# Weight-block sums formed in SBUF at use, instead of once in a DRAM scratch

## The chip, the cores and the metric

The kernel runs on one core of one Trainium2 chip. The metric is the device time of one execution in microseconds (us); lower is better. Three executions of the kernel before gave a median of 2685.73 us (2682.78 to 2697.74 us). A core has a matrix engine (PE, whose weight loads the profile lists apart as PEld), a vector engine (DVE), a scalar engine (ACT), a general engine (POOL), and SP, which here only starts transfers. SP's, ACT's and POOL's transfers run in queues of their own over 16 shared DMA engines.

## The reference

One layer of a decoder, for a prompt of 2048 tokens and 64 sample tokens that share all weights, all in fp32:

```python
x = x + concat([attn_o, pool_o]) @ w_out          # mixer: window attention and pooling heads
h = rmsnorm(x, g_cross); q = (h @ w_cq).reshape(...)
x = x + softmax(q @ mem_k) @ mem_v @ w_co          # cross-attention into 256 memory tokens
h = rmsnorm(x, g_ffn)
x = x + square(relu(h @ w_up)) @ w_down            # feed-forward, width 1024 -> 4096 -> 1024
y = rmsnorm(x, g_final)
```

This case is about the weights `w_up` and `w_down` of the feed-forward.

## The kernel before

**Two halves of the program.** First the mixer and the cross-attention run over the 2112 tokens in three superblocks (`superblock`); their last step, with weights `B`, adds the cross-attention's output. Then the feed-forward (`mlp`) runs over the same tokens in three segments of 704 tokens (`NSEG`, index j). Between the two, x and the normalised h are kept in DRAM (`xq`, `hq`).

**Precision.** A matrix product of fp32 operands is made of three PE products. Each operand is split into a high part, rounded by ACT to the PE's fp32r format, and the rest, which DVE or POOL subtracts; high times high, high times rest and rest times high are summed in PSUM (`mm3`; the three matmuls are lines 148 to 150).

**The feed-forward's products.** A block product of 2 x 2 blocks is done with seven products in place of eight (a Strassen scheme, indices i = 1 to 7). The hidden width is cut into eight groups g. `ups(j, g)` computes the seven up-products of a group, `downs(j, g)` the seven down-products of it; the order is `ups(j, 0)`, then `ups(j, g)`, `downs(j, g-1)` in turn, so a **pair** is seven up- and seven down-products. The eighth group's down-part (`down_last`) uses plain blocks. One product is 24 matmuls. Each of the seven takes a weight tile of 128 x 1024 (512 KB): for i = 3 and 4 a raw block of the weight, for i = 7, 2, 5 and 6 a sum of two blocks, for i = 1 a difference. Activations have such sums too: `hsplit` makes those of the hidden layer, with a POOL addition where one is needed (line 1452), an ACT rounding (line 1455) and a DVE subtraction (line 1456). The two hidden buffers `HC` take turns, so the split for the product after the next waits until PE has finished with its buffer.

**Where the weight tiles come from.** For each of 15 weight groups (8 up, 7 down) the scratch `us_s` or `ds_s` holds all seven tiles. They are made once, by `Work`: six copies DRAM to DRAM on SP's queue (line 1724), four transfers on POOL's queue that add a second block into the copied one (line 1726), and one difference, which is loaded into SBUF, subtracted by DVE (line 1703) and stored. `Work.step` issues the next of these at fixed places of the program: through the second and third superblock, the cross-attention, and on into the first feed-forward segment (after most products with j = 0).

**The stream of weights.** `Stream` hands out weight tiles in the order of use. There are ten SBUF tiles (`WS`), two per item: the raw tile becomes the rest, a second takes the rounded high part. `emit` issues the load (line 174), the ACT rounding (line 175) and the subtraction (line 176, on DVE; on POOL for i = 5 and 1 of the down-products) in one go, up to five items ahead (`pump`), as soon as tiles are given back. Instructions run in order on each engine, so ACT's rounding of a tile stands in ACT's queue from the moment the item is emitted.

**What sets the order.** The program is recorded in Python's order, then a scheduler moves instructions by their dependences; what is wrapped in `keep_in_program_order` keeps its place among its like. The places shown below are read from the built program.

## Time and profile before

| | |
|---|---|
| median of three runs | 2685.73 us (2682.78 to 2697.74) |
| the profiled execution | 2693.55 us, span 2691.8 us |
| PE, DVE, ACT, POOL busy | 92%, 68%, 47%, 29% of the span |
| bytes moved by DMA | 468.26 MB, of them 31.46 MB in POOL's queue |
| transfers POOL issues that add into `us_s`, `ds_s` | 32 and 28 of 512 KB |
| feed-forward segments | three, from about 1256, 1780 and 2236 us; the last runs to the end |

The span is the profiler's, from the first to the last instruction. A row of the stages view gives for a stretch of time the busy time of each engine, in brackets its number of instructions, then the clock that PE was granted as a share of full speed, the share of the 16 DMA engines' time and the rate moved. The timeline gives start, duration, engine, line and, in brackets, how long the engine was idle before and what ended it. In the DMA view a row of issues ends with the median time from issue to landing.

### The profile page before, as it was taken

The page shows a single profiled execution, that of the slowest core. Times are in us where ns is not written, and L with a number is a line of the kernel's source. Part 1 is how long each engine was busy: PE and PEld are TensorE (multiplying, and loading weights), DVE is VectorE, ACT ScalarE, POOL GpSimd, SP SyncE. Part 2 cuts the span into 40 slices and gives each one's busy share as a digit, 9 for nine tenths or more (in the row PEclk, how much of TensorE's full clock was granted, in tenths as well). Part 3 has the DMA queues.
Part 4 walks back from the last instruction along what each step waited for, and adds up shares of the span by engine and source line. Part 5 has one row for each costly group of instructions (what it writes and reads, how often), then busy time and mean ns, then how long its engine had stood idle before and what let it go on. Part 6 is the DMA issues. An engine that isn't in the chain of part 4 may idle for free.

```text
span 2691.8 us, 38281 instructions
## 1 busy us (share of the span) xinstructions
PE 2474.4 (92%) x14655; PEld 2332.1 (87%) x14655; DVE 1840.2 (68%) x2591; ACT 1252.2 (47%) x2055; POOL 788.1 (29%) x713
## 2 busy tenths in 40 slices
PE   7899989679999889997898989899999989999997
PEld 7798868678979779667888979899999989999997
DVE  6568264558455556647667658987787898787787
ACT  5666234337244344434544334545545545544542
POOL 3215224315334224211422312133322214222220
PEclk9999999889999889998999989999999999999998
DMA  7841525763736947476876623463433436433331
GB/s 244 256 143 53 213 102 189 242 192 108 233 123 200 295 135 246 169 276 216 275 225 208 227 94 137 163 206 134 138 137 133 159 125 213 138 135 133 135 140 67
DMA packets 167275, 468.26 MB, mean 174 GB/s; under 512 B 22852, under 2 KB 85252, under 8 KB 161540
## 3 DMA queue, kind: packets, MB, share of 16 engines
q1 hardware_dynamic: 149620, 417.05, 44.2%
q0 software_dynamic: 4800, 31.46, 6.4%
q10 hardware_dynamic: 12672, 17.30, 1.8%
q8 instruction: 115, 1.88, 0.3%
q14 instruction: 68, 0.56, 0.1%
HBM read 417.90 MB, written 135.94 MB: 206 GB/s over the span
## 4 chain that ended last, share of the span: by engine, by line
PE 56%; DVE 20%; DMA 10%; ACT 5%; issue 4%; POOL 3%; SPq 0%; ACTq 0%; DVEq 0%; POOLq 0%
PE d L149 11%; PE d L150 11%; PE d L148 11%; PE mm L337 5%; PE mm L336 5%; PE mm L335 4%; DVE w L176 4%; DVE act L1456 3%; ACT w L175 2%; DMA w<-us_s 2%; DMA w<-ds_s 2%; DVE x L1488 2%; PE mm L150 2%; PE mm L149 2%; PE mm L148 2%
## 5 line engine op out<-in xcount | busy, mean ns | idle before, releaser
L148 PE MATMUL d<-act,w 128*128 128x352 f32 x2552 | 834.4, 328 | 38.1 <-ACT w L175 17.6
L150 PE MATMUL d<-act,w 128*128 128x352 f32 x2552 | 833.4, 327 | 1.9 <-DVE w L176 1.9
L149 PE MATMUL d<-act,w 128*128 128x352 f32 x2488 | 813.0, 327 | 15.1 <-DVE act L1456 14.1
L175 ACT CAST w<-w 128x1024 fp32r<-128x1024 f32 x411 | 430.0, 1049 | 630.5 <-DMA w<-us_s 275.1
L176 DVE TENSOR_TENSOR w<-w,w 128x1024 fp32r<-128x1024 f32 x369 | 497.2, 1350 | 234.7 <-ACT w L175 232.0
L148 PEld LDWEIGHTS d<-act,w 128*128 128x128 f32 x2552 | 485.8, 191 | 45.2 <-ACT w L175 19.5
L149 PEld LDWEIGHTS d<-act,w 128*128 128x128 f32 x2488 | 477.3, 192 | 27.2 <-DVE act L1456 26.0
L150 PEld LDWEIGHTS d<-act,w 128*128 128x128 f32 x2552 | 487.5, 191 | 3.5 <-DVE w L176 3.4
L335 PE MATMUL mm<-act,w 128*128 128x384 f32 (+2 forms) x1248 | 414.9, 333 | 37.5 <-ACT w L175 29.5
L337 PE MATMUL mm<-act,w 128*128 128x384 f32 (+2 forms) x1248 | 410.4, 329 | 3.3 <-DVE w L176 3.1
L336 PE MATMUL mm<-act,w 128*128 128x384 f32 (+2 forms) x1248 | 408.8, 328 | 0.1
L335 PEld LDWEIGHTS mm<-act,w 128*128 128x128 f32 x1248 | 241.7, 194 | 44.5 <-ACT w L175 31.3
L337 PEld LDWEIGHTS mm<-act,w 128*128 128x128 f32 x1248 | 241.8, 194 | 9.8 <-DVE w L176 5.5
L336 PEld LDWEIGHTS mm<-act,w 128*128 128x128 f32 x1248 | 242.0, 194 | 3.1 <-DVE act L701 0.4
L259 POOL TENSOR_TENSOR t<-t,t 128x384 f32<-128x384 f32 (+2 forms) x133 | 149.0, 1122 | 279.2 <-ACT t L258 273.2
L1452 POOL TENSOR_TENSOR fb<-fb 128x704 f32<-128x704 f32 x65 | 131.5, 2029 | 289.1 <-DVE act L1456 269.1
L176 POOL TENSOR_TENSOR w<-w,w 128x1024 fp32r<-128x1024 f32 x42 | 103.1, 2455 | 357.5 <-ACT w L175 357.1
L1488 DVE TENSOR_TENSOR x<-d,x 128x704 f32<-128x704 f32 x210 | 181.6, 883 | 21.4 <-PE d L150 21.3
L1452 POOL TENSOR_TENSOR fr<-fr 128x704 f32<-128x704 f32 x40 | 81.4, 2034 | 148.1 <-DVE act L1456 137.6
L150 PE MATMUL mm<-w,act 128*128 128x512 f32 x288 | 115.8, 402 | 6.7 <-DVE act L290 4.8
L148 PE MATMUL mm<-w,act 128*128 128x512 f32 x288 | 114.9, 403 | 7.4 <-ACT act L288 5.1
L149 PE MATMUL mm<-w,act 128*128 128x512 f32 x288 | 114.8, 399 | 3.5 <-DVE w L176 3.5
(291 smaller groups left out, 3730.9 us busy)
## 6 DMA issues: line engine op xcount, KB each, us to landing
w<-us_s SPq DMA_DIRECT2D x168, 512.0 KB, 3.3
w<-ds_s SPq DMA_DIRECT2D x147, 512.0 KB, 3.2
us_s<-in_wup SPq DMA_DIRECT2D x48, 512.0 KB, 7.2
ds_s<-in_wdn SPq DMA_DIRECT2D x42, 512.0 KB, 7.2
us_s<-in_wup POOLq DMA_DIRECT2D x32, 512.0 KB, 8.2
ds_s<-in_wdn POOLq DMA_DIRECT2D x28, 512.0 KB, 7.1
w<-a_s SPq DMA_DIRECT2D x24, 512.0 KB, 5.1
w<-b_s SPq DMA_DIRECT2D x24, 512.0 KB, 3.6
```

The lines of the kernel that those rows point to most:

```text
L148: nc.tensor.matmul(ps, Wh(k), Hh(k), start=first and i == 0, stop=False)
L149: nc.tensor.matmul(ps, Wh(k), Hl(k), start=False, stop=False)
L150: nc.tensor.matmul(ps, Wl(k), Hh(k), start=False, stop=final and i == last)
L175: i1 = nc.scalar.copy(th[:], r[:, 0:1024])
L176: i2 = eng.tensor_tensor(tl[:], r[:, 0:1024], f32(th[:]), ALU.subtract)
L259: nc.gpsimd.tensor_tensor(self.acc[:, 0:n], self.acc[:, 0:n], t[:, 0:n], ALU.add)
L335: nc.tensor.matmul(ps[:, 0:n], w8(th)[:, k, :], hi(b, k), start=k == 0, stop=False)
L336: nc.tensor.matmul(ps[:, 0:n], w8(th)[:, k, :], lo(b, k), start=False, stop=False)
L337: nc.tensor.matmul(ps[:, 0:n], w8(tl)[:, k, :], hi(b, k), start=False, stop=k == 7)
L1452: nc.gpsimd.tensor_tensor(pre[0], pre[0], pre[1], pre[2])
L1456: nc.vector.tensor_tensor(lo, src, f32(hi), ALU.subtract)
L1488: nc.vector.tensor_tensor(r, v2(d), r, ALU.add)
```

## The change

The scratch now holds four raw blocks per group instead of seven finished tiles. They are copied there once, as are the other scratch weights, by 39 transfers on POOL's queue, two 512 KB blocks at a time, at every other call of `Work.step`; no sum or difference is made ahead, and none of `Work`'s transfers is left in the feed-forward. The feed-forward's items go through a new stage `pipe`: SP loads the first block; at the next `pump` POOL issues a transfer that adds the second block into the SBUF tile (`add_on`); two pumps later the tile is split as before (`split`). For i = 1 both blocks are loaded, into the two tiles of the item, and DVE forms the difference through a scratch of 704 and one of 320 columns (`DT`), ACT rounds it and DVE subtracts. Over the program that is 180 adding transfers into SBUF and 45 second loads. At most two items are held split (`RDY`), six in all (`DEPTH`).

```diff
-WIX = {3: 0, 7: 1, 2: 2, 4: 3, 5: 4, 6: 5, 1: 6}
+WSUM = {3: (0,), 4: (3,), 7: (1, 3), 2: (2, 3), 5: (0, 1), 6: (2, 0), 1: (0, 3)}
+RDY, DEPTH, CAGE = 2, 6, 2
...
-    us_s = drp.tile([8, 7, P, 1024], F32, name="us_s", tag="us_s")
-    ds_s = drp.tile([7, 7, P, 1024], F32, name="ds_s", tag="ds_s")
+    us_s = drp.tile([8, 4, P, 1024], F32, name="us_s", tag="us_s")
+    ds_s = drp.tile([7, 4, P, 1024], F32, name="ds_s", tag="ds_s")
...
             if key[0] in ("us", "ds"):
                 assert work.ready(key[0][0], key[2]), key
+                tl = WS.get()
+                nc.sync.dma_start(f32(tl[:]), raw[0])
+                th = None
+                if key[3] == 1:
+                    th = WS.get()
+                    nc.sync.dma_start(f32(th[:]), raw[1])
+                    raw = raw[:1]
+                self.pipe.append([key, tl, raw[1:], eng, 0, th])
+                return
...
+        def add_on(self, e):
+            for src in e[2]:
+                tc.keep_in_program_order(nc.gpsimd.dma_start(f32(e[1][:]), src, accum_op=ALU.add))
+            e[2] = ()
+
+        def split(self):
+            key, tl, raw, eng, n, th = self.pipe.popleft()
+            if th is not None:
+                for t, c in zip(DT, (slice(0, 704), slice(704, 1024))):
+                    nc.vector.tensor_tensor(t, f32(tl[:, c]), f32(th[:, c]), ALU.subtract)
+                    nc.scalar.copy(th[:, c], t)
+                    nc.vector.tensor_tensor(tl[:, c], t, f32(th[:, c]), ALU.subtract)
+            else:
+                th = WS.get()
+                nc.scalar.copy(th[:], f32(tl[:]))
+                eng.tensor_tensor(tl[:], f32(tl[:]), f32(th[:]), ALU.subtract)
+            self.ready.append((key, th, tl))
+
         def pump(self):
-            while self.items and len(WS.free) - 2 >= self.resW and len(self.ready) < 5:
+            for e in self.pipe:
+                e[4] += 1
+                if e[2]:
+                    self.add_on(e)
+                    e[4] = 1
+            while self.pipe and self.pipe[0][4] > CAGE and len(self.ready) < RDY and WS.free:
+                self.split()
+            while self.items:
+                if self.items[0][0][0] in ("us", "ds"):
+                    if len(WS.free) < 2 + self.resW or len(self.pipe) + len(self.ready) >= DEPTH:
+                        break
...
-                if j == 0 and i not in (3, 6):
-                    work.step()
...
-                cp_ = [("c", o[g, i], w[g, b], None) for i, b in enumerate((0, 1, 2, 3, 0, 2))]
-                ac = [("a", o[g, i], w[g, b], (k, g) if i == 5 else None) for i, b in ((1, 3), (2, 3), (4, 1), (5, 0))]
...
+                self.units += [(o[g, 2 * h:2 * h + 2], w[g, 2 * h:2 * h + 2], (k, g) if h else None) for h in range(2)]
...
         def step(self, go=True):
...
+            if go and self.units:
+                self.odd += 1
+                if self.odd % 2:
+                    self.unit()
```

The built program shows where the new instructions stand. Below, w0 to w9 are the ten weight tiles, act6 and act7 the two hidden buffers, fb and fr the hidden groups, d0 to d3 the PSUM tiles; a wait on DMAHW is one on a transfer that SP issued, on DMASW one that POOL issued. Both places are in the second segment, at `downs` of the fourth group.

ACT, the last five hidden roundings (L1455) of that group and the weight roundings (L175) between them, before:

```order
L1455 CAST act6_66<-fb1_87 128x704 [waits PE_49]
L175 CAST w6_82<-w1_77 128x1024 [waits DMAHW2_49]
L1455 CAST act7_67<-fb1_87 128x704 [waits PE_49]
L175 CAST w4_80<-w8_84 128x1024 [waits DMAHW3_49]
L1455 CAST act6_66<-fb1_87 128x704 [waits DVE_49,PE_49,Pool_49]
L175 CAST w5_81<-w9_85 128x1024 [waits DMAHW4_49,Pool_49]
L1455 CAST act7_67<-fb1_87 128x704 [waits DVE_49,PE_49]
L175 CAST w0_76<-w3_79 128x1024 [waits DMAHW5_49]
L1455 CAST act6_66<-fb1_87 128x704 [waits DVE_49,PE_49,Pool_49]
```

and after the change, the same five (now L1492) with the weight roundings (now L207):

```order
L1492 CAST act6_66<-fb1_87 128x704 [waits PE_49]
L1492 CAST act7_67<-fb1_87 128x704 [waits PE_49]
L1492 CAST act6_66<-fb1_87 128x704 [waits DVE_49,PE_49,Pool_49]
L207 CAST w3_79<-w8_84 128x1024 [waits DMASW5_49,Pool_49]
L1492 CAST act7_67<-fb1_87 128x704 [waits DVE_49,PE_49]
L207 CAST w4_80<-w5_81 128x1024 [waits DMASW6_49,PE_49]
L1492 CAST act6_66<-fb1_87 128x704 [waits DVE_49,PE_49,Pool_49]
L207 CAST w7_83<-w1_77 128x1024 [waits DMAHW6_49,DMASW7_49]
```

Before, a weight rounding that waits for an SP load stands ahead of each hidden rounding. Now two do, and they wait for an adding transfer: those of the down-weights i = 7 (DMASW5) and i = 6 (DMASW6). The third (DMASW7) is the next group's up-weight i = 2.

POOL, from the same group on, before (L1452 hidden additions, L176 weight subtractions):

```order
L1452 TENSOR_TENSOR fb1_87<-fb1_87 128x704 [waits DVE_49,Pool_49] x2
L176 TENSOR_TENSOR w9_85<-w9_85,w5_81 128x1024 [waits DMAHW7_49,PE_49,Activation_49]
L1452 TENSOR_TENSOR fr4_13382<-fr4_13382 128x704 [waits Activation_49] x2
L176 TENSOR_TENSOR w7_83<-w7_83,w2_78 128x1024 [waits DMAHW1_49,PE_49,Activation_49]
L1452 TENSOR_TENSOR fb1_87<-fb1_87 128x704 [waits DVE_49]
```

and after (L195 adding transfers, L1489 hidden additions, L208 a weight subtraction):

```order
L195 DMA w5_81<-ds_s_95 128x1024 [waits DMAHW2_49,DMASW3_49,PE_49]
L195 DMA w3_79<-ds_s_95 128x1024 [waits DMAHW4_49,PE_49]
L1489 TENSOR_TENSOR fr4_13337<-fr4_13337 128x704 [waits Activation_49]
L208 TENSOR_TENSOR w3_79<-w3_79,w9_85 128x1024 [waits DMASW4_49,Activation_49]
L1489 TENSOR_TENSOR fr4_13337<-fr4_13337 128x704 [waits Activation_49]
L195 DMA w8_84<-ds_s_95 128x1024 [waits DMAHW0_49,DMASW5_49,PE_49]
L195 DMA w5_81<-ds_s_95 128x1024 [waits DMAHW1_49,DMASW6_49,PE_49]
L1489 TENSOR_TENSOR fb1_87<-fb1_87 128x704 [waits DVE_49]
L195 DMA w1_77<-us_s_94 128x1024 [waits DMAHW2_49,DMASW7_49,PE_49]
L195 DMA w9_85<-us_s_94 128x1024 [waits DMAHW4_49,DMASW0_49,PE_49]
L195 DMA w5_81<-us_s_94 128x1024 [waits DMAHW0_49,DMASW1_49,PE_49]
```

POOL's queue loses one of its two weight subtractions in a pair and gets eight adding transfers. In the rows shown, ds_s rows are the down-weights i = 2, 5, then 7 and 6; us_s rows the up-weights i = 2, 5 and 7 of the next group. Each waits for its SP load, and the hidden additions stand between them.

More of the change, by code (lines that the diff above doesn't have):

```diff
@@ L1490, in downs @@
                     flush()
-                    if pp == 0 and j == 0 and i != 6:
-                        work.step()
                 WS.put(th, tl)
@@ L1669, in __init__ @@
             grp = [(k, g) for g in range(8) for k in "ud"][:-1]
-            self.units, self.made = [], set()
-            self.diffs = [(us_s if k == "u" else ds_s, io["wup"] if k == "u" else io["wdn"], g) for k, g in grp]
-            one = [("c", win_s[2 * g:2 * g + 2], io["win"][2 * g:2 * g + 2], None) for g in range(5)]
-            one += [("c", wo_s[4 * h:4 * h + 4, :, 0:512], io["woa"][4 * h:4 * h + 4], None) for h in range(2)]
-            prev = []
+            self.made = set()
+            self.units = [(win_s[2 * g:2 * g + 2], io["win"][2 * g:2 * g + 2], None) for g in range(5)]
@@ L1686, in __init__ @@
-                prev = ac
-            self.units += [("c", dn_s[h:h + 1], io["wdl"][h:h + 1], None) for h in range(4)]
-            self.units += prev
-            self.n = 0
-            self.tile = None
-            self.job = None
-            self.more = True
+                self.units += [(o[g, 2 * h:2 * h + 2], w[g, 2 * h:2 * h + 2], (k, g) if h else None) for h in range(2)]
+            self.units += [(dn_s[2 * h:2 * h + 2], io["wdl"][2 * h:2 * h + 2], None) for h in range(2)]
+            self.odd = 0
@@ L1694, in ready @@
         def ready(self, k, g):
-            return (k, g) in self.made and all(not (d[2] == g and d[0] is (us_s if k == "u" else ds_s)) for d in self.diffs)
+            return (k, g) in self.made
         def step(self, go=True):
-            self.n += 1
-            if self.job:
-                (o, w, g), at = self.job
-                t = self.tile
-                if self.n - at == DLAG:
-                    tc.keep_in_program_order(nc.vector.tensor_tensor(t[:, 0:1024], t[:, 0:1024], t[:, 1024:2048], ALU.subtract))
-                elif self.n - at == DLAG + 1:
-                    tc.keep_in_program_order(nc.sync.dma_start(o[g, 6], t[:, 0:1024]))
-                    self.job = None
-                    if not self.more:
-                        self.tile = None
-            elif self.tile is not None and self.diffs and go:
-                x = self.diffs.pop(0)
-                o, w, g = x
-                for i in range(2):
-                    tc.keep_in_program_order(nc.sync.dma_start(self.tile[:, 1024 * i:1024 * i + 1024], w[g, 3 * i]))
-                self.job = (x, self.n)
-                return
```

49 lines of the change are left out of this document (15 added, 34 removed).

## The prediction

> **What bounds the kernel now.** I read the page's busy times and slices first, then the stages view over the feed-forward, then waits and timeline where a stage falls short.
>
> ```profile
> PE 2474.4 (92%) x14655; PEld 2332.1 (87%) x14655; DVE 1840.2 (68%) x2591; ACT 1252.2 (47%) x2055; POOL 788.1 (29%) x713
> PEclk9999999889999889998999989999999999999998
> DMA  7841525763736947476876623463433436433331
> q0 software_dynamic: 4800, 31.46, 6.4%
> ```
>
> PE is busy for 92% of the span, nearly always at its full clock, so time is won only where PE waits. The stages show where (columns: stretch, length, then PE, PEld, DVE, ACT, POOL, then clock, DMA share, GB/s):
>
> ```profile
> 1283.00:1306.00 23.00, 16.04 (x85) 15.29 (x84) 12.75 (x9) 10.10 (x12) 15.08 (x10) 0.85 1.03 341
> 1306.00:1760.30 454.30, 415.80 (x2417) 404.17 (x2416) 334.26 (x338) 204.28 (x240) 117.61 (x69) 0.95 0.55 178
> 1760.30:2214.50 454.20, 444.91 (x2722) 439.06 (x2721) 372.06 (x387) 230.65 (x272) 125.73 (x60) 0.99 0.44 151
> 1400.00:1420.00 20.00, 16.31 (x88) 15.25 (x87) 14.76 (x17) 8.24 (x10) 0.85 (x2) 0.91 0.76 233
> 1540.00:1600.00 60.00, 46.52 (x221) 43.51 (x220) 23.98 (x23) 21.52 (x25) 12.94 (x7) 0.80 0.33 111
> 1555.00:1560.00 5.00, 3.70 (x11) 3.24 (x12) 1.22 (x1) 0.94 (x2) 0.00 (x0) 0.50 0.01 2
> 1720.00:1740.00 20.00, 14.34 (x81) 12.71 (x80) 20.00 (x25) 10.88 (x13) 0.00 (x0) 0.98 0.58 193
> ```
>
> The second and third rows are stretches of equal length in the first and the second segment. The first does 2417 matmuls, the second 2722: 305 x 454.2 / 2722 = 51 us of PE work missing. Ahead of it, 23 us hold 85 matmuls where the second segment's rate gives 138: 9 more. In the second segment, away from the change of segments, nothing is left to win; the sum of fourteen 10-us stages from 1880 to 2020 us reads
>
> ```profile
> sum 140.00, PE 139.72 PEld 138.54 DVE 110.56 ACT 70.30 POOL 39.31; mean PE 9.98 PEld 9.90 DVE 7.90 ACT 5.02 POOL 2.81
> ```
>
> So a pair of 14 products (24 matmuls each, 14 x 24 x 454.2 / 2722 = 56 us with the change of segments in it; 52.5 us at the full rate of 64 in 10 us) is PE's. What the first segment lacks, the timeline shows in one place:
>
> ```profile
> 1398.08 0.32 SPq L174 DMA_DIRECT2D w<-us_s  x1
> 1398.44 0.49 SPq L1724 DMA_DIRECT2D us_s<-in_wup  x1
> 1402.03 1.04 ACT L175 CAST w<-w 128x1024 fp32r<-128x1024 f32 x1 [7.01 <-DMA w<-ds_s]
> 1402.98 0.77 ACT L1455 CAST act<-fb 128x704 fp32r<-128x704 f32 x1
> ```
>
> ACT stood 7.01 us in a weight's rounding, behind it the hidden rounding that PE's next product needed, with a scratch copy between the loads on SP's queue. The waits view says how common that is over the run (time, count, mean), and the DMA view of 1290 to 1560 us, against that from 1780 us on, how much slower a load lands beside the copies:
>
> ```profile
> ACT w L175 <- DMA w<-us_s: 275.1, 131, 6.9
> ```
>
> ```profile
> q1 hardware_dynamic: 9989, 48.57, 48.4%
> q0 software_dynamic: 1680, 11.01, 21.4%
> w<-us_s SPq DMA_DIRECT2D x30, 512.0 KB, 4.6
> us_s<-in_wup POOLq DMA_DIRECT2D x11, 512.0 KB, 8.3
> ds_s<-in_wdn POOLq DMA_DIRECT2D x10, 512.0 KB, 7.9
> ```
>
> ```profile
> q1 hardware_dynamic: 43735, 129.30, 41.2%
> w<-us_s SPq DMA_DIRECT2D x106, 512.0 KB, 3.2
> ```
>
> **A, the first segment.** 25 copies and 25 adding transfers leave it, and its load landings should fall from 4.6 to 3.2 us. At most the whole 60 us come back. At least none, since the row of 1540 to 1600 us loses much with almost nothing of the copies left: 221 matmuls where the second segment's rate gives 360, so 60 x 139 / 360 = 23 us, with the 16 engines a third busy and at 1555 idle (0.01). Whether that slow stretch is an after-effect of the copies the rows don't show. I take the other 60 - 23 = 37 whole and a third of the 23: **-45**.
>
> **B, the mixer.** Its chain of waits has writes and loads that take far longer than their like (start, length):
>
> ```profile
> 521.34 7.55 DMA xq<-x
> 539.04 19.65 DMA xq<-x
> 562.77 15.46 DMA hq<-x
> 867.86 8.24 DMA w<-win_s
> 905.38 10.90 DMA hq<-x
> 944.75 8.32 DMA w<-win_s
> 985.76 6.04 DMA w<-win_s
> ```
>
> ```profile
> x<-xq SPq DMA_DIRECT2D x12, 704.0 KB, 4.9
> w<-us_s SPq DMA_DIRECT2D x168, 512.0 KB, 3.3
> ```
>
> Over 4.9 us for the four of x and h and 3.3 for the three weights that is 2.7 + 14.8 + 10.6 + 6.0 + 4.9 + 5.0 + 2.7 = 47 us. Ahead of the feed-forward some 65 copies, 39 adding transfers and 45 loads and stores of differences go, and 60 copied blocks come. A load costs 0.412 x 910 / 129.3 x 0.524 = 1.52 us of the 16 engines' time (share, stretch and megabytes of the row above); an adding transfer 0.064 x 2691.8 / 60 = 2.87. So 65 x 1.52 + 39 x 2.87 + 45 x 1.52 = 279 us fall to 60 x 1.52 = 91. Bounds 0 and -47; two thirds of the load goes, but the 1 MB transfers come in bursts and some of these waits have another cause: **-23**.
>
> [...]
>
> **C, the weight's way in the feed-forward.** Here the change adds. Per pair 14 loads become 16, and eight adding transfers come: 14 x 1.52 = 21.3 us of the 16 engines become 16 x 1.52 + 8 x 2.87 = 47.3 of 52.5, or 90%. These still fit. What counts is whether each lands in time. I followed the ten tiles through the program's order: the tightest item is the down-weight i = 7, whose tile comes free when the product of i = 2 ends and which is used four products later, 4 x 24 / 64 x 10 = 15.0 us; the others have five or more. Its rounding stands on ACT ahead of the hidden rounding of its own product (the order shown above). From the 15.0 come off, after the landing, the weight's rounding, the hidden rounding and the hidden subtraction (like L1488 in size), from the groups of 1780 to 2236 us:
>
> ```profile
> L175 ACT CAST w<-w 128x1024 fp32r<-128x1024 f32 x110 | 115.5, 1050 | 166.1 <-DMA w<-us_s 90.4 <-DMA w<-ds_s 67.2 <-DMA w<-dn_s 7.2
> L1488 DVE TENSOR_TENSOR x<-d,x 128x704 f32<-128x704 f32 x70 | 60.6, 883 | 6.3 <-PE d L150 6.3
> L176 POOL TENSOR_TENSOR w<-w,w 128x1024 fp32r<-128x1024 f32 x14 | 34.3, 2451 | 108.7 <-ACT w L175 108.6
> L176 DVE TENSOR_TENSOR w<-w,w 128x1024 fp32r<-128x1024 f32 x95 | 125.6, 1322 | 30.9 <-ACT w L175 30.8
> ```
>
> 15.0 - 1.05 - 0.77 - 0.88 = 12.3 us. The load takes 3.2, POOL's issue about 0.9 (rows below), so the adding transfer has 8.2 us; the ones of before, DRAM to DRAM, took 8.3 and 7.9. No margin. Into SBUF no row exists: from below 3.2 (a load), lateness 0; from above the loads' own rise under traffic. They go from 3.2 to 4.6 us when the share goes from 0.41 to 0.70; to 0.90 by the same slope 5.5, and 8.1 x 5.5 / 4.6 = 9.7. Late by 9.7 - 8.2 + 5.5 - 3.2 = 3.8 us, 21 x 3.8 = 80. I take 1 us per pair, nearer the lower end since one of its two memory ends is now SBUF: **+21** (0 to +80).
>
> DVE gets, for each i = 1, 2 x (0.88 + 0.40) = 2.56 us in place of 1.32 (up) and of POOL's 2.45 (down): 1.24 + 2.56 = 3.8 us per pair, from 79% (110.56 of 140) to 86%. It stays hidden behind PE; without that cover it would be 21 x 3.8 = 80 us, which is inside C's end. POOL gets 8 issues of some 0.9 us, less 2.45:
>
> ```profile
> 1288.35 7.86 POOL L1502 TENSOR_TENSOR x<-x 128x704 f32<-128x704 f32 x4 [39.47 <-DMA x<-xq]
> 1309.81 0.74 POOL L1726 DMA_DIRECT2D us_s<-in_wup  x1
> 1330.84 1.06 POOL L1726 DMA_DIRECT2D us_s<-in_wup  x1
> ```
>
> At 39.31 of 140 us that is hidden too.
>
> **D and E, the edges.** At a change of segments the x loads, the y stores and the plain blocks of `down_last` meet the adding transfers, and DVE is full there already (1720): 0 to +30, **+10** for both changes. At the start the first up-weights' adding transfers queue on POOL behind L1502, which waited 39.47 us for x; the raw blocks i = 3 and 4 cover two products: **+3**.
>
> **Sum.** -45 - 23 + 21 + 10 + 3 = -34 us: the profiled execution's 2693.55 becomes 2659.6. The median of the runs lies 7.8 below that execution, so I say **2652**.
>
> **Rivals.** *R1, the adding transfer is late* (slower). It lands after 8.2 us at the down-weight i = 7; ACT waits there, the hidden rounding behind it comes late and PE stops once a pair. All else gives -55, so it decides from 55 / 21 = 2.6 us per pair. At the 3.8 of above plus 1.0, because i = 6 and the next group's i = 2 follow in the same queue, it is 4.8 x 21 = 101, sum +46, 2732. For it: the zero margin and the 90%. Against: the tiles are handed out by use, and a late pair takes no more than the slots allow.
>
> [...]
>
> *R2, the gain is hidden anyway.* The first segment loses by the start of its own pipeline, not by the copies (the rows at 1540 and 1555), and the mixer's long writes keep their length beside the 1 MB transfers. Then A and B shrink to a third, -23, against 13 and C: 2697 with C at 21, 2676 with none; I write 2686.
>
> *R3, the sums never reach the clock*: since all loads were hidden in segments two and three, only A and B count and C, D, E are 0: -68, 2618. It is the good end of the forecast.
>
> **Numbers.** Forecast with R3 .55, R1 .27, R2 .18. The range reaches from 2605, where A is all of its 60 and B half-way to 47 with no loss, to 2735, R1's price: about one in ten lies outside at each end. The forecast's own range is 2615 to 2675. A measurement of this kernel tells 0.5%, 13 us, from no change: 2672 to 2699. Faster .53 (the forecast's cases but a few), same .18, slower .29.
>
> **What would show it.** A: the first segment as long as the second, its ACT waits on SP loads near zero. B: the named writes at 5 to 8 us. C: adding transfers of the feed-forward landing in 6 to 8 us, and PE above 9.9 of 10 in the second segment's middle. R1: gaps on PE released by ACT or DVE once per pair at `downs`, ACT's L207 waiting on the POOL queue. R2: the first segment still short of matmuls with no copies in it. I am wrong altogether if DVE or POOL's queue, not a landing, sets the pace.

## The result, and the profile after

The changed kernel is slower: 2877.3 us median (2876.64 to 2877.69) against 2687.59 us (2682.78 to 2697.74), a ratio of 1.070 (95% interval 1.0669 to 1.0732). The forecast was 2652 and its range ended at 2735. From the page of the changed kernel (profiled execution 2877.69 us):

```profile
PE 2517.1 (88%) x14655; PEld 2362.4 (82%) x14655; DVE 1938.9 (67%) x2732; ACT 1251.8 (44%) x2100; POOL 844.4 (29%) x851
PEclk9999899888989889998899999999999998999998
DMA  7832332442432443377787888588888858878872
q0 software_dynamic: 27648, 135.28, 21.7%
```

PE does the same 14655 matmuls in 184 us more. The DMA row shows both halves of the change as planned: the 16 engines are emptier in the mixer (slices 4 to 16) and twice as busy in the feed-forward. So the time can be laid out by matmuls: both traces have the same number, and the time from the n-th to the m-th start is taken from each (us), from the first matmul to the last.

| matmuls | place | before | after | difference |
|---|---|---|---|---|
| 0 to 2500 | start, first superblock | 504.2 | 496.7 | -7.5 |
| 2500 to 4500 | second superblock | 409.2 | 512.6 | **+103.4** |
| 4500 to 6500 | rest of the mixer | 341.5 | 342.0 | +0.5 |
| 6500 to 7000 | change to the feed-forward | 98.6 | 107.3 | +8.7 |
| 7000 to 9000 | first segment | 372.2 | 353.1 | -19.1 |
| 9000 to 9500 | change of segments | 89.3 | 111.7 | +22.4 |
| 9500 to 11500 | second segment | 323.4 | 345.4 | +22.0 |
| 11500 to 12500 | change of segments | 175.9 | 205.7 | +29.8 |
| 12500 to the end | third segment | 358.5 | 382.8 | +24.3 |

More than half of the loss lies in the second superblock, which none of the prediction's loss terms named. The stages view of that stretch, before and then after:

```profile
512.00:921.20 409.20, 366.00 (x2001) 338.88 (x2001) 241.56 (x486) 174.16 (x401) 138.99 (x180) 0.96 0.62 195
```

```profile
504.40:1017.00 512.60, 392.20 (x2002) 350.40 (x2002) 247.88 (x488) 186.91 (x428) 150.62 (x206) 0.89 0.37 127
```

Nearly the same work on each engine, DMA share down from 0.62 to 0.37 as term B had it, and still 103 us more. PE is idle for 120 us in place of 43, and busy for 26 us more at a lower granted clock (0.89, before 0.96). PE's longest waits in the two stretches (what it waited for, then time, count, longest), before and then after:

```profile
PE aux L745 <- DVE act L137: 13.5, 2, 8.9
PE aux L268 <- POOL t L259: 8.9, 3, 7.4
```

```profile
PE mm L381 <- ACT act L334: 38.4, 6, 19.1
PE aux L314 <- POOL t L305: 24.6, 4, 14.8
PE aux L791 <- DVE st L792: 18.5, 7, 8.9
```

None is a wait on a transfer of the copies. L305 adds up the squares of the mixer's normalisation and L334 rounds what it yields for the next dense product; L791 and L792 are attention's scores.

In the feed-forward PE stops once a pair. The chain of waits of the changed kernel at one such stop (start, length):

```profile
1991.47 6.50 DMA w<-ds_s
1998.06 0.13 DVE dt L202
1998.19 1.58 issue
1999.77 2.69 DVE x L202
2002.46 0.80 DVE x L1525
2003.26 1.82 DVE w L208
2005.09 0.80 DVE x L1525
2005.88 0.81 DVE act L1493
```

This is the down-weight i = 1: its second load waited until 1991.47 for a tile from PE and took 6.50 us; then the two parts of the difference (L202) stood on DVE's queue ahead of the hidden subtraction (L1493) that PE needed. The view has "issue" where the engine waited for nothing that the profile shows. PE then ran at a granted clock of 0.52 (stages view):

```profile
2003.00:2006.70 3.70, 0.43 (x1) 0.19 (x1) 3.70 (x5) 1.31 (x2) 2.74 (x3) 0.97 0.84 269
2006.70:2010.00 3.30, 3.26 (x11) 3.26 (x12) 3.30 (x5) 0.00 (x0) 0.00 (x0) 0.52 0.97 192
```

The landings and shares behind it, from the DMA view of the 9500th to the 11500th matmul after the change:

```profile
q1 hardware_dynamic: 14132, 50.29, 41.7%
q0 software_dynamic: 6781, 24.68, 38.6%
w<-us_s SPq DMA_DIRECT2D x48, 512.0 KB, 4.9
w<-ds_s SPq DMA_DIRECT2D x47, 512.0 KB, 5.5
w<-us_s POOLq DMA_DIRECT2D x24, 512.0 KB, 7.9
w<-ds_s POOLq DMA_DIRECT2D x23, 512.0 KB, 8.8
```

### The profile page after: what moved, and what is told of

Its sections match the earlier page's. It is cut to its first block, busy times and chain, and to the rows that moved or that the text cites. A ratio compares the mean times of both kernels' runs of the same rounds, so it can differ in the third digit from the quotient of the medians.

```text
span 2875.9 us, 38733 instructions
## 1 busy us (share of the span) xinstructions
PE 2517.1 (88%) x14655; PEld 2362.4 (82%) x14655; DVE 1938.9 (67%) x2732; ACT 1251.8 (44%) x2100; POOL 844.4 (29%) x851
## 4 chain that ended last, share of the span: by engine, by line
PE 55%; DVE 18%; DMA 13%; ACT 5%; issue 4%; POOL 4%; SPq 0%; ACTq 0%; POOLq 0%; DVEq 0%
PE d L150 10%; PE d L151 10%; PE d L149 10%; PE mm L383 5%; PE mm L381 5%; PE mm L382 5%; DMA w<-ds_s 5%; DMA w<-us_s 2%; PE mm L149 2%; PE mm L150 2%; DVE w L208 2%; PE mm L151 2%; DVE x L1525 2%; DVE w L187 2%; POOL t L305 2%
## 5 line engine op out<-in xcount | busy, mean ns | idle before, releaser
L149 PE MATMUL d<-act,w 128*128 128x352 f32 x2552 | 845.3, 332 | 60.8 <-ACT w L207 46.3
L150 PE MATMUL d<-act,w 128*128 128x352 f32 x2488 | 820.5, 330 | 48.8 <-DVE act L1493 48.8
L151 PE MATMUL d<-act,w 128*128 128x352 f32 x2552 | 841.1, 330 | 6.0 <-DVE w L208 5.9
L149 PEld LDWEIGHTS d<-act,w 128*128 128x128 f32 x2552 | 494.3, 194 | 69.0 <-ACT w L207 48.3
L150 PEld LDWEIGHTS d<-act,w 128*128 128x128 f32 x2488 | 484.8, 195 | 55.7 <-DVE act L1493 55.0
L151 PEld LDWEIGHTS d<-act,w 128*128 128x128 f32 x2552 | 495.2, 194 | 10.4 <-DVE w L208 10.3
L381 PE MATMUL mm<-act,w 128*128 128x384 f32 (+2 forms) x1248 | 416.0, 336 | 80.0 <-ACT act L334 38.4
L208 DVE TENSOR_TENSOR w<-w,w 128x1024 fp32r<-128x1024 f32 x249 | 350.1, 1412 | 136.3 <-ACT w L207 134.7
L207 ACT CAST w<-w 128x1024 fp32r<-128x1024 f32 x270 | 278.2, 1048 | 371.8 <-DMA w<-us_s 167.2
L383 PE MATMUL mm<-act,w 128*128 128x384 f32 (+2 forms) x1248 | 412.0, 331 | 3.8 <-DVE w L187 3.8
L381 PEld LDWEIGHTS mm<-act,w 128*128 128x128 f32 x1248 | 244.7, 197 | 91.5 <-ACT act L334 40.4
L305 POOL TENSOR_TENSOR t<-t,t 128x384 f32<-128x384 f32 (+2 forms) x133 | 141.8, 1074 | 415.1 <-ACT t L304 409.8
L383 PEld LDWEIGHTS mm<-act,w 128*128 128x128 f32 x1248 | 243.8, 195 | 10.6 <-DVE w L187 5.9
L382 PEld LDWEIGHTS mm<-act,w 128*128 128x128 f32 x1248 | 244.9, 196 | 7.7 <-DVE act L336 3.4
L195 POOL DMA_DIRECT2D w<-us_s x96 | 84.6, 917 | 442.9 <-DVE act L1493 202.1
L186 ACT CAST w<-w 128x1024 fp32r<-128x1024 f32 x96 | 100.5, 1049 | 239.1 <-DMA w<-a_s 99.4
L187 DVE TENSOR_TENSOR w<-w,w 128x1024 fp32r<-128x1024 f32 x96 | 121.9, 1276 | 113.4 <-ACT w L186 113.1
L1525 DVE TENSOR_TENSOR x<-d,x 128x704 f32<-128x704 f32 x210 | 181.6, 882 | 5.5 <-PE d L151 4.2
L1489 POOL TENSOR_TENSOR fb<-fb 128x704 f32<-128x704 f32 x65 | 128.9, 1984 | 156.9 <-ACT fb L1441 109.6
L195 POOL DMA_DIRECT2D w<-ds_s x84 | 80.5, 981 | 183.7 <-DMA w<-ds_s 165.1
L149 PE MATMUL mm<-w,act 128*128 128x512 f32 x288 | 116.9, 410 | 12.2 <-ACT act L334 8.6
```

The source lines that it names most:

```text
L149: nc.tensor.matmul(ps, Wh(k), Hh(k), start=first and i == 0, stop=False)
L150: nc.tensor.matmul(ps, Wh(k), Hl(k), start=False, stop=False)
L151: nc.tensor.matmul(ps, Wl(k), Hh(k), start=False, stop=final and i == last)
L187: i2 = eng.tensor_tensor(tl[:], r[:, 0:1024], f32(th[:]), ALU.subtract)
L195: tc.keep_in_program_order(nc.gpsimd.dma_start(f32(e[1][:]), src, accum_op=ALU.add))
L207: nc.scalar.copy(th[:], f32(tl[:]))
```

## The experiments

Times of runs without an interval are of one execution each; the kernel before ran beside them at 2691 to 2698. A stretch below is the time between two matmuls, as in the table.

### The two halves apart

The mixer of before with the feed-forward of the change (e1), and the reverse (e2). Each edit puts one kernel's `Work` and its calls in the mixer into the other; the lines below show which blocks its feed-forward then reads, for e1 against the change, then for e2 against before, where it also no longer calls `Work`:

```diff
-                    S.add(("us", j, g, i), *[us_s[g, b] for b in WSUM[i]])
+                    S.add(("us", j, g, i), *[us_s[g % 4, b] for b in WSUM[i]])
```

```diff
-                    S.add(("us", j, g, i), us_s[g, WIX[i]])
+                    S.add(("us", j, g, i), us_s[g, WIX[i] % 4])
...
-                if j == 0 and i not in (3, 6):
-                    work.step()
```

> The feed-forward of the change behind the mixer of before: `Work` is that of before, with its copies, adding transfers and differences in the mixer, and PE's order of the mixer is row for row that of before. What `Work` has left at the feed-forward's start is not issued; the feed-forward reads, in the change's way, blocks of the scratch that are filled by then, so the output is not the layer's. After the change the 4500th matmul starts 96 us later than before, and 96 us later still at the feed-forward's start. Theory O (the mixer's loss is the mixer's own, from `Work` on POOL's queue and the order that the scheduler makes with it): the feed-forward starts at about 1260 us and the whole takes 2877 - 96 = 2781. Rival F (the feed-forward's new way costs the mixer something, by tiles or by loads pulled ahead): the mixer stays long, 2830 to 2877.

> The other half: the mixer and `Work` of the change (PE's order of the mixer is row for row the change's), and a feed-forward as before, one load and one split per item, but with nothing of `Work` in it and no sums (each item reads one raw block, so the output is not the layer's). Theory O: the mixer ends 96 us late; the first segment is as long as the second, so term A shows alone: 2687 + 96 - 50 = 2733, between 2720 and 2750. Rival: were the first segment's loss its own, 2783. If the mixer is as before, theory O falls and the time is 2637.

Measured: 2787.47 and 2749.53. From the 2500th to the 4500th matmul the first takes 410.5 us, the second 513.3: the loss goes with the mixer, and rival F (the new feed-forward costs the mixer something) falls. The second run also gives term A cleanly. The first segment of before, and of the second run:

```profile
1361.29:1733.53 372.24, 343.89 (x2002) 334.77 (x2001) 266.62 (x273) 167.94 (x196) 94.86 (x53) 0.94 0.54 176
```

```profile
1446.47:1777.88 331.41, 325.13 (x2001) 320.77 (x2001) 268.00 (x273) 168.04 (x196) 85.97 (x40) 1.00 0.44 142
```

That is 41 us, and 11.5 more between matmuls 6500 and 7000: 52 us in place of the 45 taken. With nothing of `Work` in it the segment keeps no slow stretch like that of 1540 to 1600 us, which so was an after-effect of `Work`. And the whole feed-forward of the change costs 1506 us from the 6500th matmul on, that of the second run 1378: forming the sums at use costs 128 us.

### What of the sums costs

```diff
-            for src in e[2]:
-                tc.keep_in_program_order(nc.gpsimd.dma_start(f32(e[1][:]), src, accum_op=ALU.add))
             e[2] = ()
```

> The change with the 180 adding transfers into SBUF left out (the items i = 7, 2, 5 and 6 hold their first block alone, so the output is not the layer's); loads, pumps, and the two loads and the difference of i = 1 as they are. A pair of the second segment takes some 56.2 us after the change, against 52.5. Theory D1 (the pair waits for the down-weight i = 1: its second load waits for a tile that PE gives back late, and then comes DVE, ACT, DVE twice): the pair stays at 55 to 56 us, the whole at 2850 to 2877. Rival R (the adding transfers land late or slow the loads, as R1 of the prediction had it): the pair falls to 52.5 and the whole by 21 x 3.7 = 78 and some of the change of segments, 2770 to 2800.

2751.51, below rival R's range too: theory D1 falls as it was put. Without adding transfers the feed-forward takes 1385 us, so they make 121 of the 128, and the second loads and differences some 8. (A pair of the second segment takes 345.4 x 336 / 2000 = 58.0 us after the change, 54.3 before, 55.0 here; the 56.2 and 52.5 of the expectation were too low.) The place of the stop was right: PE still stops there once a pair, but for 1.0 us instead of 2.6, and SP's `ds_s` loads now land in 4.3 us.

```diff
                 if key[3] == 1:
+                    raw = raw[:1]
+                if key[3] == 99:
```

> The change with i = 1 taken from one block: one load, one rounding and one subtraction as for i = 3 (45 second loads and the differences left out, so the output is not the layer's); the 180 adding transfers stay. Theory D1: the pair falls to 52.5 to 53.5 us, the whole by 60 to 80: 2797 to 2817. Rival R: the pair stays at 55 to 56 us, the whole at 2860 to 2877.

2918.32, beyond both. With the second block the edit had also sent the subtraction of i = 1 back to POOL, so it was repeated with that left on DVE:

```diff
                 if key[3] == 1:
+                    raw = raw[:1]
+                if key[3] == 99:
...
-                    S.add(("ds", j, g - 1, i), *[ds_s[g - 1, b] for b in WSUM[i]], eng=nc.gpsimd if i in (5, 1) else None)
+                    S.add(("ds", j, g - 1, i), *[ds_s[g - 1, b] for b in WSUM[i]], eng=nc.gpsimd if i == 5 else None)
```

> The run with i = 1 from a single block, which was 41 us slower than the change, moved the down-weight's subtraction of i = 1 to POOL with the same edit (as before the change). Here it stays on DVE: the change without second loads and differences, and nothing else (output not the layer's). Theory D1: the pair falls from 58 us to 53 or 54, the whole to 2800 to 2830. Theory P (the ring over POOL: an adding transfer is issued behind a subtraction or a hidden addition on POOL, which waits for ACT's rounding of an earlier item, which waits for that item's adding transfer): i = 5's subtraction is still on POOL, the pair stays at 56 to 58, the whole at 2855 to 2890.

2924.6, again beyond both ranges. D1 is refuted, but neither does theory P foresee a loss against the change: what the second loads cost stays at the 8 us of above. PE now stops two to three times a pair; the chain of waits at one stop shows a ring over POOL:

```profile
2020.04 6.16 DMA w<-ds_s
2026.27 1.06 ACT w L209
2027.41 2.40 POOL w L210
2029.81 1.57 POOL fr L1491
2031.43 1.35 POOL fr L1491
2032.78 1.28 issue
2034.06 1.79 POOL w L197 x2
2038.58 1.66 POOL fb L1491
2040.23 7.53 DMA w<-us_s
2047.78 1.06 ACT w L209
2053.20 0.89 DVE act L1495
```

An adding transfer lands (6.16), ACT rounds, POOL subtracts (L210, i = 5), does the hidden additions queued behind it (L1491), and only then issues the next adding transfers (L197), of which the third lands 7.53 us later, late for PE. In the change one hidden addition stands between that subtraction and the next two issues, here two do: leaving one load out had moved them. That this move makes all of the 47 us over the change isn't shown. Two edits take one link out each. First the transfer's own time:

```diff
-                tc.keep_in_program_order(nc.gpsimd.dma_start(f32(e[1][:]), src, accum_op=ALU.add))
+                tc.keep_in_program_order(nc.gpsimd.dma_start(f32(e[1][:]), src))
```

> The change with each of the 180 adding transfers made a plain one of the same block on the same queue (it overwrites the tile, so the output is not the layer's): same instructions, same order, same bytes from the scratch. Adding transfers land in 7.8 to 8.4 us, SP's plain loads in 4.8 to 5.6. Theory R (landing time and load on the 16 engines): landings of 4 to 5 us, 16 x 1.5 of 52.5 us and 8 x 1.5 more (70%), the pair at 53 to 54 us, the whole at 2770 to 2800. Theory P, or the issue on POOL: the pair stays at 56 us or more, the whole above 2840.

2811.97, just over R's range; the 9500th to the 11500th matmul takes 328.1 us (before 323.4, change 345.4). Its DMA view there:

```profile
q0 software_dynamic: 6765, 24.64, 20.9%
w<-us_s SPq DMA_DIRECT2D x48, 512.0 KB, 3.8
w<-us_s POOLq DMA_DIRECT2D x24, 512.0 KB, 5.7
```

One plain transfer takes 0.209 x 328.1 / 47 = 1.46 us of the 16 engines, an adding one 0.386 x 345.4 / 47 = 2.84. With the same instructions in the same order, the adding itself costs 68 of the 121 us (1506 less 1438 from the 6500th matmul on), nearly all of what the middles of the segments lose. The other 53, which plain transfers cost as well, lie at the edges; by what there, no run shows. Then POOL's link:

```diff
-                    S.add(("ds", j, g - 1, i), *[ds_s[g - 1, b] for b in WSUM[i]], eng=nc.gpsimd if i in (5, 1) else None)
+                    S.add(("ds", j, g - 1, i), *[ds_s[g - 1, b] for b in WSUM[i]], eng=None)
```

> The change with the down-weight's subtraction of i = 5 moved from POOL to DVE; nothing else. Theory P (the adding transfers are issued late because POOL's queue stands in that subtraction, which waits for ACT's rounding of a tile whose own adding transfer has to land): the stretch of the 9500th to the 11500th matmul falls from 345 us to 330 to 338, the whole to 2810 to 2850. Theory R (the landing of 8 us itself against 5.5 of a plain transfer, in front of the product at which PE waits once a pair): 343 to 350, the whole at 2870 to 2890.

2851.21, 26 us less than the change; the stretch takes 339.8, between the two expectations. So POOL's subtraction costs something, and the adding itself more. How it costs isn't told apart: with it on DVE the transfers behind it no longer wait for it, but neither does POOL subtract any more while DVE forms the difference of i = 1, whose 320-column part (L202) takes 0.52 us in the mean of the run's 45, in the change 1.22 (2.69 in five of the twelve in this stretch, see the last section).

### What of the mixer costs

The scheduler gave the change another order of the whole mixer. Some of PE's rows of the second superblock in the program as built, before the change (L335 to L337 are the dense products, L745, L711, L776 the attention's; the number ahead counts rows, in the trace the first is the 2765th matmul):

```
2605 L335 MATMUL mm_125<-act_62,w_81 128x384
2606 L336 MATMUL mm_125<-act_64,w_81 128x384
2607 L745 MATMUL aux_132<-mc_4051,act_60 128x256 x2
2608 L337 MATMUL mm_125<-act_62,w_85 128x384
2609 L711 MATMUL aux_131<-ident,fb_86 128x128
2610 L745 MATMUL aux_129<-mc_4051,act_61 128x256 x2
2611 L335 MATMUL mm_125<-act_63,w_81 128x384
```

and after (L381 to L383 dense; L822, L791, L839, L840 attention; the first is the 2873rd matmul of the trace):

```
2702 L382 MATMUL mm_128<-act_63,w_82 128x384
2703 L383 MATMUL mm_128<-act_63,w_77 128x384
2704 L822 MATMUL aux_130<-ident,x_91 128x128 x4
2705 L822 MATMUL aux_131<-ident,x_91 128x128 x4
2706 L791 MATMUL aux_132<-mc_4009,act_61 128x256 x2
2707 L839 MATMUL mm_127<-act_68,vt 128x512
2708 L822 MATMUL aux_130<-ident,x_91 128x128
```

Before, a dense matmul stands between the attention's small ones, whose operands come through ACT, DVE and POOL; after, the dense ones run out and the small ones follow each other. A count of this: how often PE's order, in rows 2300 to 4300, changes between products with a weight and other matmuls. Five runs vary order and traffic. First the copies cut to 16 of 128 rows:

```diff
-                self.units += [(o[g, 2 * h:2 * h + 2], w[g, 2 * h:2 * h + 2], (k, g) if h else None) for h in range(2)]
+                self.units += [(o[g, 2 * h:2 * h + 2, 0:16], w[g, 2 * h:2 * h + 2, 0:16], (k, g) if h else None) for h in range(2)]
```

> The change with the 30 transfers that copy raw blocks cut to 16 of 128 rows: as many instructions on POOL, an eighth of the bytes; the feed-forward reads its blocks from the mixer's own weight scratch in place of the missing ones, so the output is not the layer's. PE's order of the mixer is the change's in 96% of the first 6300 rows (70% with before). Between the 2500th and the 4500th matmul before takes 409 us, the change 513. Theory T (the traffic of the 1 MB copies makes the mixer slow): 410 to 440. Theory O2 (the order that the scheduler makes: PE changes between the dense products and the attention's small ones 90 times in rows 2300 to 4300, 154 times before, and stands in the attention's rings in between; here 104 times): 490 to 515.

Copies on SP:

```diff
-            tc.keep_in_program_order(nc.gpsimd.dma_start(dst, src))
+            tc.keep_in_program_order(nc.sync.dma_start(dst, src))
```

> The change with `Work`'s copies issued by SP in place of POOL, the same 1 MB transfers at the same places. The scheduler makes another order again: 70 changes between dense and attention products in those rows, and one stretch of 180 small matmuls with no dense one between. Theory O2: the 2500th to the 4500th matmul takes as long as in the change or longer, 510 to 560. Theory Q (what costs is that POOL's queue carries the copies): 410 to 450.

No copies of raw blocks:

```diff
-                self.units += [(o[g, 2 * h:2 * h + 2], w[g, 2 * h:2 * h + 2], (k, g) if h else None) for h in range(2)]
+                self.made.add((k, g))
```

> The change without the 30 transfers that copy raw blocks (the feed-forward reads blocks of the mixer's own scratch, so the output is not the layer's). The scheduler's order of the mixer comes back near that of before: 142 changes between dense and attention products in rows 2300 to 4300 (before 154, the change 90, copies cut to an eighth 104). Measured so far from the 2500th to the 4500th matmul: before 409 us, cut copies 481, the change 513, copies on SP (70 changes) 527. Theory O2: 410 to 425. If the order told nothing, 480 as with the cut copies.

Copies on ACT:

```diff
-            tc.keep_in_program_order(nc.gpsimd.dma_start(dst, src))
+            tc.keep_in_program_order(nc.scalar.dma_start(dst, src))
```

> The change with `Work`'s copies issued by ACT in place of POOL: the same 1 MB transfers at the same places of the program. The scheduler's order of rows 2300 to 4300 has 120 changes between dense and attention products, the longest stretch of small matmuls 41 (the change 90 and 55, on SP 70 and 180, without copies 142 and 14). Theory O2: the stretch of the 2500th to the 4500th matmul comes between the 399 us without copies and the 513 of the change, 440 to 480. Theory T (traffic alone): 505 to 530, as with the two other queues.

Single blocks at every step:

```diff
-                self.units += [(o[g, 2 * h:2 * h + 2], w[g, 2 * h:2 * h + 2], (k, g) if h else None) for h in range(2)]
+                self.units += [(o[g, h:h + 1], w[g, h:h + 1], (k, g) if h == 3 else None) for h in range(4)]
...
-                if self.odd % 2:
+                if True:
```

> The change with the raw blocks copied one at a time (512 KB, 60 transfers on POOL's queue) at every step in place of two at every other: the same bytes over the same places. The order has 59 changes, the longest stretch of small matmuls is 76. Theory O2: 515 to 550 us from the 2500th to the 4500th matmul. Theory T: the smaller pieces at an even pace are milder, 440 to 500.

| kernel | changes in the order | copies in the mixer | matmuls 2500 to 4500, us | whole, us |
|---|---|---|---|---|
| before | 154 | 62, and 41 adding transfers | 409 | 2692 |
| e9 | 142 | no raw blocks | 399 | 2763 |
| o1 | 120 | all, on ACT | 428 | 2788 |
| e5 | 104 | an eighth | 481 | 2843 |
| change | 90 | all, on POOL | 513 | 2877 |
| e6 | 70 | all, on SP | 527 | 2896 |
| o2 | 59 | all, in halves | 548 | 2921 |

But for the first two rows, whose times differ by 10 us, the count ranks the stretch, from 399 us to 548, and traffic doesn't: an eighth of it costs 481 in one order, all of it 428 in another. Nor are those 10 us the copies': two runs of the next section (d1, d3) have 142 changes too, with a DMA share of 0.62 in the stretch where e9 has 0.30, and take 401 and 397 us.

One row has another cause in it. With the copies on SP (e6), PE waits in the stretch for ACT's roundings and DVE's subtractions of weights for 79 us, in the change for 2. So its place in the ranking says little for the order, and it doesn't refute theory Q, that POOL's queue is what costs. The change's trace speaks against Q: POOL issues 29 copies in the stretch, in 0.52 us each, with no wait before any, 15 us in all.

The stages view of the run without raw copies, and of the last:

```profile
507.06:905.95 398.89, 365.14 (x2001) 337.54 (x2001) 251.87 (x510) 189.09 (x430) 135.47 (x176) 0.96 0.30 99
```

```profile
509.58:1057.79 548.21, 408.17 (x2001) 365.12 (x2001) 248.03 (x493) 189.33 (x433) 161.86 (x228) 0.84 0.34 115
```

At nearly one DMA share, 149 us apart. The figures of e9, e5 and o1 lie 11, 9 and 12 us under the ranges given for them. The traffic's own part is not told apart from the order exactly; e5 and the change, whose orders agree in 96% of the rows, differ by 31 us, and the other 72 of the 103 stay with an eighth of the bytes. That the count itself is the cause, and not the places on ACT and POOL that the scheduler moved with it, isn't shown: no run has the change's copies in the order of before. Why the scheduler gives one order or the other is open: the five edits of the copies gave five.

Both losses lessened at once, copies on ACT and i = 5 on DVE:

> The change with both edits that helped singly: `Work`'s copies issued by ACT (2788 us alone) and the down-weight's subtraction of i = 5 on DVE (26 us less alone). The order of the mixer is that of the copies on ACT. If the two losses are separate: 2762, between 2752 and 2772. What stays over before is then the adding transfers' landing and the changes of segments.

2753.24, 124 us under the change, where the two make 89 and 26 singly: they add up, within 9 us. What remains over before lies in the feed-forward, 1489 us from the 6500th matmul on against 1418; up to there this run is 12 us faster than before.

### Can term A be had

A says that 52 us hang on the copies in the first segment. Five runs leave the sums as they were before and only issue `Work` earlier, without the change:

```diff
-                work.step(len(qdone) > 2)
+                work.step(4 * (len(qdone) > 2) if s == 2 else len(qdone) > 2)
```

The diff is of c2; c1 has 2 in place of 4 there, and 3 after the window attention of the third superblock.

> The kernel before, correct in its output, with `Work` stepped two times per place in the third superblock's first products and three times after its window attention: 86 of 94 copies and 56 of 60 adding transfers lie ahead of the feed-forward, 62 and 41 before. PE's order of the second superblock is that of before (154 changes). The run with no copies and no sums in the feed-forward had its first segment 52 us shorter than before. If the mixer pays nothing: 2687 - 40 = 2647; if each moved transfer costs its 1.5 to 2.9 us of the 16 engines in the mixer's chain: 2687 - 40 + 24 x 1.5 + 15 x 2.9 = 2726. I expect 2650 to 2670.

> The kernel before, correct in its output, with `Work` stepped four times per place in the third superblock's first products: all copies and adding transfers lie ahead of the feed-forward, in bunches. The feed-forward's first segment should be as in the run with nothing of `Work` in it, 52 us shorter; the bunches cost more of the third superblock than the spread ones: 2640 to 2680, and above c1 if bunching decides.

c1 2716.74 (1.009, interval 1.0059 to 1.0121), c2 2695.15 (0.9997, 0.9983 to 1.0011), both over what was expected: the first segment is short (330.9 and 329.9 us from the 7000th to the 9000th matmul), and the third superblock longer by 38 and 47 us; c1 loses 15 more at the change to the feed-forward, c2 wins 12 there. The stretch of matmuls 4500 to 6500 in before and in c2:

```profile
921.20:1262.69 341.49, 303.16 (x2001) 254.29 (x2001) 200.26 (x431) 146.18 (x327) 96.99 (x136) 0.93 0.64 206
```

```profile
923.13:1311.88 388.75, 316.22 (x2001) 263.82 (x2001) 198.15 (x431) 147.14 (x327) 115.29 (x158) 0.89 0.80 244
```

c2 gives back 47 of some 55 us where the DMA share was 0.64 already. In the first superblock it was 0.52 (0 to 512 us):

```diff
-            if s:
-                work.step(len(qdone) > 2)
+            work.step(2 * (len(qdone) > 2) if s == 0 else len(qdone) > 2)
```

The diff is of d3; d1 has one step there, d5 three.

> The kernel before, correct in its output, with `Work` stepped in the first superblock's products too: 73 copies and 48 adding transfers ahead of the feed-forward (62 and 41 before). The order of the second superblock has 142 changes (before 154, without copies 142 too). If the first superblock hides them: 2688 less a third of 52, 2665 to 2680. If they cost there what they cost elsewhere: 2680 to 2695.

> As the run above, with two steps per place in the first superblock: 84 copies and 56 adding transfers ahead of the feed-forward, 142 changes. If the first superblock hides them: 2645 to 2665. If they cost there what they cost elsewhere: 2680 to 2700.

> The kernel before, correct in its output, with three steps of `Work` per place in the first superblock's products: nothing of `Work` is left in the feed-forward (10 copies and 4 adding transfers were with two steps, 0.986 of before). The first segment can lose 4 us more between the 7000th and 9000th matmul and some 15 ahead of it; the first superblock gets 10 copies more. 2640 to 2665.

d1 2696.39 (1.0005, 0.999 to 1.0021), d3 2658.15 (0.9862, 0.9841 to 0.9882), d5 2655.24 (0.9864, 0.9813 to 0.9915). d1 lies just over the range of the case in which the transfers cost there what they cost elsewhere, d3 and d5 in the ranges of the case in which they are hidden. d3 and d5 are faster than before by 1.4%, with intervals below 1: some 37 us. In d3 the start to the 2500th matmul costs 9.7 us more, the second superblock 12 less, the first segment takes 334.9 us. Why one step (d1) brings nothing, with 359.6 us in the first segment and 20.7 more at the start, isn't told apart by these runs; 21 copies are left in the first segment, against 32 before and 10 in d3.

## Why the prediction was wrong, by its steps

In the prediction's terms, the 184 us between the traces are -52 (A, taken -45), +96 (B, taken -23), +85 (C, taken +21) and +43 (D and E, taken +13); 12 more the feed-forward of e2 loses after its first segment, which no run explains.

- **What bounds the kernel, and A, right.** The first segment lost 52 us to `Work` (e2); 45 were taken. The rival R2, that it loses by its own pipeline, is refuted. (Its rows show 21 adding transfers, not the 25 that it names; the sum doesn't use the number.)
- **B, wrong, and the step that decided.** It priced the mixer by its DMA share and the excess of seven transfers, with everything else standing still, and took -23. The share fell as said, but the scheduler reordered the mixer: -7.5, +103.4 and +0.5. That a change of `Work` can change PE's order there was put at nothing, and the orders shown ahead of the result are of the feed-forward alone. The excess of the named transfers was worth little either: without the raw blocks' copies the stretch gains 10 us (e9), about as much as with the transfers of before in d1 and d3, where the bound was 47 for the mixer.
- **C, the mechanism half right, the size four times too small.** The 2.87 us of engine time for an adding transfer came out as 2.84, its 8.1 us of landing as 7.9 and 8.8, the load's 3.2 as 4.9 and 5.5 against the 5.5 worked out. By its own working such landings make 8.8 - 8.2 + 5.5 - 3.2 = 2.9 us per pair (3.8 with the 9.7 that it allowed for), and 3.7 was measured (58.0 less 54.3); as the stop is at another place, that these are so near is luck. Without the edges forming the sums costs 128 - 43 = 85 us, over the +80 of its bound. Wrong was to take 1 us "since one of its two memory ends is now SBUF": no row said so. The place was wrong as well: not the rounding of i = 7 on ACT, but the difference of i = 1 on DVE, which waits for a tile and a second load. "It stays hidden behind PE" counted DVE's share and not what is queued behind its waits.
- **POOL, missed.** Its eight issues were summed up as busy time. They stand behind a subtraction that waits for an earlier adding transfer. Taking that subtraction off POOL is worth 26 us (e10), of which some may be DVE's, as said there.
- **D and E, right in sign, too small.** +13 were forecast. Against e2, which has no sums, the 500 matmuls at the start lose 20.2 us, the two changes 18.0 and 28.0; less 3.8 x 2000 / 336 = 23 for the pairs in these stretches, it is 43.
- **R1, nearest of the rivals.** That adding transfers are what costs at use was right; its place (i = 7, on ACT) wasn't, so that its 101 for the pairs lies near the 85 is luck in part. Its total of 2732 lacks the mixer's 96 and more.
- **The clock at the stop.** At the stop shown, after 3.70 us with one matmul, the granted clock was 0.52 for 3.30 us, which costs an estimated 3.3 x 0.48 = 1.6 us. The sum has no term for this.

## What to carry to other kernels

Where a scheduler orders the program, compare the order of PE in every phase, the ones the diff doesn't mean to touch too, before pricing traffic: here a count of how finely two kinds of matmul are interleaved ranked the kernels but for one pair 10 us apart. An adding transfer took the time of two plain ones on the engines here (2.84 against 1.46 us), and its issue stood on POOL's queue behind subtractions and additions besides: ask what it stands behind, and what waits for its landing. Traffic moved out of one phase was paid in another here: of some 55 us gained, c2 gave back 47 in the third superblock; in the first superblock, d3 paid 10 us, but d1, with fewer transfers, 21.

## What was not expected of the hardware

DVE's subtractions of two SBUF operands took longer where POOL computed at the same time. The 320-column part of the i = 1 difference in the second segment (min, median, max in ns):

```profile
L202 DVE TENSOR_TENSOR x<-w,w x13: 480/483/2697, 1906.6 to 2261.9; 128x320 f32<-128x320 f32 x13
```

In the stop shown above it took 2.69 us while POOL subtracted and added:

```profile
1999.07 3.04 POOL L208 TENSOR_TENSOR w<-w,w 128x1024 fp32r<-128x1024 f32 x1
2002.08 1.93 POOL L1489 TENSOR_TENSOR fr<-fr 128x704 f32<-128x704 f32 x1
```

Over the weight subtractions on DVE (128 x 1024) from the 7000th matmul on, the median is 1.22 us for 189 with no POOL arithmetic beside them, none of them over 1.23, and 3.09 us for 25 that lie more than half under it; the additions with one operand in PSUM (L1525) take 0.88 us either way. Why they take longer there, no run shows. The prediction's 2.56 us for a difference of i = 1 left this out. What it costs the whole kernel no run tells.
